# Building the one-hot factors of the expert gates: the gate moved from B to A, and the work shared out anew among VectorE, ScalarE and GpSimd

## The chip, the cores and the metric

The kernel runs on one core of one Trainium2 chip. The time is the device time of one execution in microseconds (us); the number given for a kernel is the median of several executions.

## What is computed

The reference is one transformer block over 1024 tokens of width 1024 (16 meta tokens are put in front and dropped at the end): half of the mixing channels go through a chunked mLSTM, half through attention with a forget gate, and then comes a product-key expert layer (PEER) with 16,384 one-neuron experts. The change touches only the expert layer:

```python
def _peer(x, w_query, sub_keys, u_emb, v_emb):
    ...
        scores = jnp.einsum('thpc,hpnc->thpn', qh, keys32)
        val, idx = lax.top_k(scores, PEER_TOPK)
        ...
        top_s, pos = lax.top_k(cand, PEER_TOPK)
        ids = jnp.take_along_axis(cand_id, pos, axis=-1).reshape(tb, PEER_HEADS * PEER_TOPK)
        gate = jax.nn.softmax(top_s, axis=-1).reshape(tb, PEER_HEADS * PEER_TOPK)
        u = u_emb[ids]
        act = jax.nn.gelu(jnp.einsum('ted,td->te', u, xb).astype(jnp.float32), approximate=False)
        w = (gate * act).astype(xb.dtype)
        return jnp.einsum('te,ted->td', w, v_emb[ids])
```

Each token picks 8 heads x 16 = 128 experts. An expert's number is 128*i + j, with i and j from 0 to 127, and each pick has a gate, which is never negative because it comes out of a softmax.

## The kernel before

The 1024 tokens are four segments of 256 (two blocks of 128 each). Segments 0 and 3 take the expert layer by **gathering**: for each of a token block's 128 picks one indirect DMA, issued on GpSimd's queue (POOL), brings 128 rows of `peer_u` (tile `gu`, L329, 512 KB), and VectorE (DVE) multiplies and sums it (L338); later 128 rows of `peer_v` per token (tile `gv`, L365) are summed by TensorE (PE) into `po` (L387), four tokens per batch. The gathers of segment 0 run beside the earlier stages and are still under way in the stage looked at here; those of segment 3 are spread over the last stage by a pacer (`Paced`, L1025), each asked for after a given PE instruction.

Segments 1 and 2 (`DENSE`) take it **densely**: all 16,384 experts are computed for their 512 tokens, and the results are weighed with a matrix of gates that is zero but for the 128 picks. `gates()` (L1118) expands the picks into this matrix. It takes the i, the j and the gate of a block of 128 tokens, transposed so that a pick is a partition and a token a column (`iT`, `jT`, `gT`), and goes through the tokens in groups of four. Per token there are two 128 x 128 factors with one row per pick: A holds a 1 in column i, B the gate in column j. One matmul (L1163, tile `gout`, in fp32 two instructions in the trace) sums the product over the picks and leaves the token's 128 x 128 gates in PSUM. ScalarE (ACT) copies the four results into `G` (L1165), and every 32 tokens `G` goes to DRAM (`gd`, 2 MB). A, B and the PSUM tile `gout` have two buffers each.

Who makes what for a group of four tokens, before: DVE makes A of three tokens in one comparison of 128 x 384 (L1153); ACT makes A of the fourth in two instructions, |column - i| (L1156) and relu(1 - that) (L1157); B is made per token by one instruction that compares and multiplies by the gate (L1161), on POOL for the first token (`GPOOL = 1`) and on DVE for the other three.

What stands around it: `merge` (L1194) interleaves the expert search of segment 3 (`topk`: projections on PE, maxima on DVE), some dense projections kept for later (`spill`) and the 16 steps of `all_gates`. A scheduler then sets each engine's order for good; every engine runs its instructions in that order, so an instruction that waits holds up all behind it on its engine. After the gates comes the **last stage** (from L1216): per four rows of experts, `Gt` is read back from `gd` (L1232), multiplied into the expert activations (L1236), split into two halves `Wh` and `Wl` (L1239, L1240), and PE multiplies with `peer_v` (`vo`, L1258) between projections of `peer_u` (`du`, L293); DVE adds `vo` to the result (L1263).

Gather tiles come from two pools of 7 and 4 buffers (`GATH`, `GATHV`). For the second token block of segment 0 even batches of `gv` take the one pool and odd ones the other (`room0`, L1005).

Of the kernel before, what the change touches and what calls it, by code (L numbers as in the profile page):

```python
# [9 lines left out]
F32 = mybir.dt.float32  # L10
# [3 lines left out]
AF = mybir.ActivationFunctionType  # L14
OP = mybir.AluOpType
# [4 lines left out]
P = 128  # L20
# [25 lines left out]
DENSE = (1, 2)  # L46
# [9 lines left out]
TOP0 = (0, 1, 0, 1)  # L56
SW = 1
GP0 = 5
GACT = 1
GPOOL = 1  # L60
T3W = 1.2
GW = 1
T00 = 0
# [30 lines left out]
def _block_kernel(ctx, tc, nc, I, out, dbg):  # L94

    def pool(name, bufs, stack=ctx, **kw):
        return stack.enter_context(tc.tile_pool(name=name, bufs=bufs, **kw))
# [27 lines left out]
    def bank(name):  # L125
        turn_b[0] += 1
        if extra is not None and turn_b[0] % XB == 0:
            return extra[:, turn_b[0] // XB % 2, :]
        return ps.tile([P, 512], F32, tag="bank", name=name, bufs=2)
# [9 lines left out]
    dve, act, pe, pool_e, sync = nc.vector, nc.scalar, nc.tensor, nc.gpsimd, nc.sync  # L139
# [34 lines left out]
    iota = cp.tile([P, P], F32, tag="iota", name="iota")  # L174
# [897 lines left out]
    for i in range(-1, len(SEGS)):  # L1072
# [9 lines left out]
        if i >= 0:  # L1082
            S = segs[i]
# [34 lines left out]
    def gates(S, gb):  # L1118

        for b in range(NB):  # L1120
            hi = gb.tile([P, P], I32, tag="gi", name="gi_hi")
            lo = gb.tile([P, P], I32, tag="gi", name="gi_lo")
            dve.tensor_scalar(hi, S.idx[:, b, :], 7, None, op0=OP.logical_shift_right)
            dve.tensor_scalar(lo, S.idx[:, b, :], 127, None, op0=OP.bitwise_and)
            T = []
            for x, nm in ((hi, "iT"), (lo, "jT"), (None, "gT")):
                if x is None:
                    f = S.gate[:, b, :]
                else:
                    f = gb.tile([P, P], F32, tag="gf", name="gf", bufs=1)  # L1130
                    dve.tensor_copy(f, x)
                tb = bank("gtr")
                with tc.high_priority():
                    pe.transpose(tb[:, 0:P], f, ident)
                t_ = gb.tile([P, P], F32, tag=nm, name=nm, bufs=1)
                act.copy(t_, tb[:, 0:P])
                T.append(t_)
            iT, jT, gT = T
            if GACT:
                niT = gb.tile([P, P], F32, tag="niT", name="niT", bufs=1)  # L1140
                act.mul(niT, iT, -1.0)
            for tg in range(P // TG):
                G = gb.tile([P, P, TG], F32, tag="G", name="G")
                for q in range(TG // 4):
                    bk = dps.tile([P, 512], F32, tag="db", name="gout")
                    t0 = tg * TG + q * 4
                    ts4 = slice(t0, t0 + 4)
                    A = gb.tile([P, 4, P], F32, tag="A", name="A")
                    B = gb.tile([P, 4, P], F32, tag="B", name="B")
                    bc = [P, 4, P]  # L1150
                    io = iota.unsqueeze(1).broadcast_to(bc)
                    nd = 4 - GACT
                    dve.tensor_tensor(A[:, 0:nd], io[:, 0:nd], iT[:, t0:t0 + nd].unsqueeze(2).broadcast_to([P, nd, P]),  # L1153
                                      op=OP.is_equal)
                    for u in range(nd, 4):
                        act.activation(A[:, u, :], iota, AF.Abs, bias=niT[:, t0 + u:t0 + u + 1])  # L1156
                        act.activation(A[:, u, :], A[:, u, :], AF.Relu, bias=1.0, scale=-1.0)  # L1157
                    for u in range(4):
                        t1 = slice(t0 + u, t0 + u + 1)
                        e = pool_e if u < GPOOL else dve  # L1160
                        e.tensor_scalar(B[:, u, :], iota, jT[:, t1], gT[:, t1], op0=OP.is_equal, op1=OP.mult)  # L1161
                        with tc.high_priority():
                            pe.matmul(bk[:, u * P:(u + 1) * P], B[:, u, :], A[:, u, :], start=True, stop=True)  # L1163
                    with nullcontext():
                      act.copy(G[:, :, q * 4:q * 4 + 4].rearrange("p i t -> p t i"),  # L1165
                             bk.rearrange("p (t i) -> p t i", t=4))
                sync.dma_start(gd[(NB * (S.sg - DENSE[0]) + b) * (P // TG) + tg], G)
                yield
# [20 lines left out]
    gb = pool("gbuild", 2, gbs, reuse_waits="tile")  # L1189
    def all_gates():  # L1190
        for d in DENSE:
            yield from gates(segs[d], gb)
# [130 lines left out]
```

## Time and profile before

| | us |
|---|---|
| median of 3 runs | 3425.85 (3422.84 to 3432.39) |
| the execution that was profiled | 3424.24 |
| its span, which all times of the trace are measured in | 3422.4 |
| PE busy with matmuls | 3040.1 (89%) |
| DVE busy | 2294.6 (67%) |
| POOL busy | 1523.4 (45%) |
| ACT busy | 1066.8 (31%) |

Times of the trace count from the start of the span, which is 1.84 us shorter than the execution. A share over the whole span says little here: stages with different limits follow one another. The gates run from 1642 to 2111 us. Until 1907 PE has the projections of the search and the spill to do beside them, and from 1907 to 2111 it has only gates and gathered rows. The last stage's first `vo` matmul starts at 2128.4 and the stage lasts to the end.

A row of instructions in the profile reads: line, engine, operation, output<-inputs, shape, count | busy time, mean ns of one | idle time of the engine just before them, and what ended it. SPq is the queue of SyncE, from which most DMAs are issued.

### The profile page before, as it was taken

How to read it: one execution, taken by the hardware profiler on the slowest of the kernel's cores; microseconds unless marked ns; L12 is line 12 of the kernel's file. 1: busy time of each engine (PE TensorE's matmuls, PEld its weight loads, DVE VectorE, ACT ScalarE, POOL GpSimd, SP SyncE). 2: the span in 40 equal slices, each digit the busy share in tenths (PEclk: the TensorE clock that was granted, in tenths of full speed). 3: DMA queues.
4: the chain of work that ended last, by engine and by line, in shares of the span. 5: the costliest groups of instructions: out<-in, count | busy, mean ns of one | idle time of the engine just before them, and what ended most of it. 6: DMA issues, size and time to landing. Idle time of an engine off the chain costs nothing. (4 is left out here: it accounts for less than half of the span.)

```text
span 3422.4 us, 42278 instructions
## 1 busy us (share of the span) xinstructions
PE 3040.1 (89%) x14225; PEld 2220.2 (65%) x14225; DVE 2294.6 (67%) x5970; ACT 1066.8 (31%) x2007; POOL 1523.4 (45%) x1321
## 2 busy tenths in 40 slices
PE   8899899878768868999998775999999999999999
PEld 4566677545535646676766553777777777777666
DVE  3242678577667999776788546788767677775443
ACT  1323424233333212222444553222322232322221
POOL 1000011177875777433565675454444545444442
PEclk9998899879679888999998886999999999999999
DMA  4444445579989999866787887888889999998995
GB/s 135 131 126 137 144 145 149 167 240 315 250 299 331 328 334 346 252 242 234 283 325 280 316 302 284 287 311 314 307 310 344 345 348 343 353 342 308 339 333 205
DMA packets 373821, 931.23 MB, mean 272 GB/s; under 512 B 57268, under 2 KB 143508, under 8 KB 371556
## 3 DMA queue, kind: packets, MB, share of 16 engines
q0 software_dynamic: 161216, 552.56, 45.9%
q1 hardware_dynamic: 212388, 375.96, 32.7%
q8 instruction: 113, 1.85, 0.2%
q14 instruction: 104, 0.85, 0.1%
HBM read 860.91 MB, written 67.47 MB: 271 GB/s over the span
## 5 line engine op out<-in xcount | busy, mean ns | idle before, releaser
L329 POOL DMA_INDIRECT gu<-in_peer_u,idx x512 | 626.3, 1223 | 521.1 <-PE vo L1258 110.0
L365 POOL DMA_INDIRECT gv<-in_peer_v,idT x512 | 546.0, 1066 | 593.1 <-PE po L387 314.3
L338 DVE SCALAR_TENSOR_TENSOR gu<-gu,xng 128x1024 f32<-128x1024 f32 x472 | 592.5, 1274 | 62.5 <-DMA gu<-in_peer_u,idx 60.6
L282 ACT CAST wh<-raw 128x1024 fp32r<-128x1024 f32 x288 | 302.1, 1049 | 884.2 <-PE vo L1258 270.9
L287 DVE TENSOR_TENSOR wl<-raw,wh 128x1024 fp32r<-128x1024 f32 x262 | 320.5, 1223 | 283.0 <-ACT wh L282 250.5
L1258 PE MATMUL vo<-wh,Wh 128*128 128x512 f32 x1024 | 376.7, 396 | 34.9 <-ACT Wh L1239 18.1
L1258 PE MATMUL vo<-wl,Wh 128*128 128x512 f32 x1024 | 402.6, 393 | 0.0
L1258 PE MATMUL vo<-wh,Wl 128*128 128x512 f32 x1024 | 400.3, 392 | 0.0
L387 PE MATMUL po<-gv,Z 128*32 128x512 f32 x2048 | 262.7, 606 | 19.1 <-DMA gv<-in_peer_v,idT 18.9
L306 PE MATMUL fp<-hnh,raw 128*128 128x256 f32 (+1 forms) x1024 | 251.4, 404 | 22.3 <-DVE frs L633 11.3
L1258 PEld LDWEIGHTS vo<-wh,Wh 128*128 128x128 f32 x1024 | 194.1, 190 | 98.3 <-issue 23.3
L293 PE MATMUL du<-xl,wh 128*128 128x512 f32 x640 | 250.3, 391 | 0.0
L293 PE MATMUL du<-xh,wl 128*128 128x512 f32 x640 | 250.2, 391 | 0.0
L293 PE MATMUL du<-xh,wh 128*128 128x512 f32 x640 | 249.8, 390 | 0.0
L306 PEld LDWEIGHTS fp<-hnh,raw 128*128 128x128 f32 x1024 | 203.8, 203 | 60.5 <-DVE frs L633 12.7
L1258 PEld LDWEIGHTS vo<-wl,Wh 128*128 128x128 f32 x1024 | 193.8, 189 | 48.6 <-issue 8.4
L1258 PEld LDWEIGHTS vo<-wh,Wl 128*128 128x128 f32 x1024 | 193.2, 189 | 48.1 <-issue 7.5
L1163 PE MATMUL gout<-A,B 128*128 128x128 f32 x1024 | 164.0, 319 | 67.6 <-POOL B L1161 62.9
L1163 PEld LDWEIGHTS gout<-A,B 128*128 128x128 f32 x1024 | 150.9, 226 | 103.6 <-POOL B L1161 76.6
L1165 ACT COPY G<-gout 128x512 f32<-128x512 f32 x128 | 136.4, 1066 | 202.0 <-PE gout L1163 195.4
L433 PE MATMUL tk<-raw,hnh 128*128 128x512 f32 (+1 forms) x416 | 197.4, 623 | 2.0 <-ACT vp L576 1.8
L1263 DVE TENSOR_TENSOR acc<-acc,vo 128x512 f32<-128x512 f32 x256 | 167.0, 683 | 32.8 <-PE vo L1258 29.1
(409 smaller groups left out, 5397.5 us busy)
## 6 DMA issues: line engine op xcount, KB each, us to landing
raw<-in_ut SPq DMA_DIRECT2D x128, 512.0 KB
raw<-in_peer_v SPq DMA_DIRECT2D x128, 512.0 KB
raw<-in_wf SPq DMA_DIRECT2D x64, 512.0 KB
gd<-G SPq DMA_DIRECT2D x16, 2048.0 KB
Gt<-gd SPq DMA_DIRECT2D x32, 1024.0 KB
raw<-in_wt SPq DMA_DIRECT2D x48, 512.0 KB
raw<-in_wq SPq DMA_DIRECT2D x48, 512.0 KB
raw<-in_wo SPq DMA_DIRECT2D x32, 512.0 KB
```

The costliest lines, as they stand in the source:

```text
L282: seen["act"] = act.copy(h, raw)
L287: seen["dve"] = dve.tensor_sub(l, raw, h.bitcast(F32))
L293: seen["pe"] = pe.matmul(o, w, x[:, c], start=(first and i == 0), stop=(last and i == 2))
L306: pe.matmul(o, raw[:, k * P:(k + 1) * P], xh[:, k, c], start=(k == 0), stop=(k == KT - 1))
L329: d = pool_e.indirect_dma_start(out=t, out_offset=None, in_=I["peer_u"], in_offset=bass.IndirectOffsetOnAxis(ap=S.idx[:, lb, r:r + 1], axi ...
L338: dve.scalar_tensor_tensor(t, t, 1.0, xn[0], op0=OP.mult, op1=OP.mult, accum_out=G.actv[:, r:r + 1])
L365: d = pool_e.indirect_dma_start(out=t, out_offset=None, in_=I["peer_v"], in_offset=bass.IndirectOffsetOnAxis(ap=S.idT[lb][:, tok:tok + 1], ...
L387: last = pe.matmul(G.po[32 * q_:32 * q_ + 32, n, :], z[:, q_, 31 - j:63 - j], rows[q_][:, n * 512:(n + 1) * 512], start=(j == 0), stop=(j ...
L433: pe.matmul(b[0:w, :], xh[:, k, s0:s0 + w], raw[:, k % 2 * 512:(k % 2 + 1) * 512], start=(k == 0), stop=(k == KT - 1))
L1163: pe.matmul(bk[:, u * P:(u + 1) * P], B[:, u, :], A[:, u, :], start=True, stop=True)
L1258: seen["pe"] = pe.matmul(bks[b], w[:, cw], v, start=(ii == 0 and i == 0), stop=(ii == GRP - 1 and i == 2))
L1263: dve.tensor_add(o, o, bks[b])
```

## The change

The gate is multiplied into A, not into B. B is then a bare comparison and is made for all four tokens in one DVE instruction of 128 x 512. A is made per token: the fourth by ACT, whose second instruction now is relu(g - g*|column - i|) with the gate and the negated gate (`ngT`, new) as operands read per partition; the others by an instruction that compares and multiplies, as B was before, on POOL for the first token of a group in the first dense segment, and on DVE for the rest. In the second dense segment POOL makes nothing.

```diff
-GACT = 1
-GPOOL = 1
+
+GPOOL = (1, 0)
...
-            if GACT:
-                niT = gb.tile([P, P], F32, tag="niT", name="niT", bufs=1)
-                act.mul(niT, iT, -1.0)
+            niT = gb.tile([P, P], F32, tag="niT", name="niT", bufs=1)
+            act.mul(niT, iT, -1.0)
+            ngT = gb.tile([P, P], F32, tag="ngT", name="ngT", bufs=1)
+            act.mul(ngT, gT, -1.0)
...
-                    nd = 4 - GACT
-                    dve.tensor_tensor(A[:, 0:nd], io[:, 0:nd], iT[:, t0:t0 + nd].unsqueeze(2).broadcast_to([P, nd, P]),
-                                      op=OP.is_equal)
-                    for u in range(nd, 4):
-                        act.activation(A[:, u, :], iota, AF.Abs, bias=niT[:, t0 + u:t0 + u + 1])
-                        act.activation(A[:, u, :], A[:, u, :], AF.Relu, bias=1.0, scale=-1.0)
+                    dve.tensor_tensor(B, io, jT[:, t0:t0 + 4].unsqueeze(2).broadcast_to(bc), op=OP.is_equal)
                     for u in range(4):
                         t1 = slice(t0 + u, t0 + u + 1)
-                        e = pool_e if u < GPOOL else dve
-                        e.tensor_scalar(B[:, u, :], iota, jT[:, t1], gT[:, t1], op0=OP.is_equal, op1=OP.mult)
+                        if u == 3:
+
+                            act.activation(A[:, u, :], iota, AF.Abs, bias=niT[:, t1])
+                            act.activation(A[:, u, :], A[:, u, :], AF.Relu, bias=gT[:, t1], scale=ngT[:, t1])
+                        else:
+                            e = pool_e if u < GPOOL[S.sg - DENSE[0]] else dve
+                            e.tensor_scalar(A[:, u, :], iota, iT[:, t1], gT[:, t1], op0=OP.is_equal, op1=OP.mult)
```

Since the scheduler orders all engines anew, three places are shown. In the changed kernel the lines behind the diff are one higher. On **POOL**, at the end of the gates, there stood before (x is the number of instructions in a row; `gv` and `gu` are the gathers):

```order
L1161 TENSOR_SCALAR B<-iota,jT,gT 128x128 x6
L365 DMA gv<-in_peer_v,idT 128x1024 x5
L1161 TENSOR_SCALAR B<-iota,jT,gT 128x128
L329 DMA gu<-in_peer_u,idx 128x1024 x2
L1161 TENSOR_SCALAR B<-iota,jT,gT 128x128 x7
L365 DMA gv<-in_peer_v,idT 128x1024 x4
L1161 TENSOR_SCALAR B<-iota,jT,gT 128x128
L329 DMA gu<-in_peer_u,idx 128x1024 x3
L1161 TENSOR_SCALAR B<-iota,jT,gT 128x128
L329 DMA gu<-in_peer_u,idx 128x1024 x3
L1161 TENSOR_SCALAR B<-iota,jT,gT 128x128 x4
L329 DMA gu<-in_peer_u,idx 128x1024 x6
```

and now, from the last steps of the first dense segment on:

```order
L365 DMA gv<-in_peer_v,idT 128x1024 x7
L1162 TENSOR_SCALAR A<-iota,iT,gT 128x128
L365 DMA gv<-in_peer_v,idT 128x1024
L1162 TENSOR_SCALAR A<-iota,iT,gT 128x128 x6
L365 DMA gv<-in_peer_v,idT 128x1024 x61
L329 DMA gu<-in_peer_u,idx 128x1024 x2
L365 DMA gv<-in_peer_v,idT 128x1024 x4
L329 DMA gu<-in_peer_u,idx 128x1024 x126
```

Every factor that stood between the gathers of the second dense segment is gone, and only two `gu` stand ahead of the last four `gv`, where there were two ahead of them and seventeen more among the factors behind.

On **PE**, at the change from the gates to the last stage (`gout` here counts one instruction a token, `po` eight a batch of four tokens; `idt` are two small transposes), before:

```order
L1163 MATMUL gout<-A,B 128x128 x5
L387 MATMUL po<-gv,Z_139 32x512 x6
L1163 MATMUL gout<-A,B 128x128 x3
L387 MATMUL po<-gv,Z_139 32x512 x2
L1163 MATMUL gout<-A,B 128x128 x16
L387 MATMUL po<-gv,Z_141 32x512 x8
L1163 MATMUL gout<-A,B 128x128 x8
L360 MATMUL idt<-identr,idf 128x128
L1163 MATMUL gout<-A,B 128x128 x8
L360 MATMUL idt<-identr,idf 128x128
L1163 MATMUL gout<-A,B 128x128 x20
L1258 MATMUL vo<-wh,Wh 128x512
```

and now:

```order
L387 MATMUL po<-gv,Z_139 32x512 x8
L1164 MATMUL gout<-A,B 128x128 x26
L387 MATMUL po<-gv,Z_141 32x512 x8
L1164 MATMUL gout<-A,B 128x128 x4
L387 MATMUL po<-gv,Z_139 32x512 x8
L1164 MATMUL gout<-A,B 128x128 x38
L387 MATMUL po<-gv,Z_141 32x512 x8
L387 MATMUL po<-gv,Z_139 32x512 x8
L387 MATMUL po<-gv,Z_141 32x512 x8
L387 MATMUL po<-gv,Z_139 32x512 x8
L1259 MATMUL vo<-wh,Wh 128x512
```

The gates now end before the gathered rows: four batches of `po` stand between the last gate and the first `vo`, where before the gates were last. From the last `du` of the search part on there are 17 batches and 67 groups of four tokens before, 16 batches and 64 groups now.

On **DVE**, at the same change of stage (`gu` is the gathered product of segment 3, `Z` a small copy for a batch of `po`), before:

```order
L1153 TENSOR_TENSOR A<-iota,iT 128x384
L1161 TENSOR_SCALAR B<-iota,jT,gT 128x128 x3
L338 SCALAR_TENSOR_TENSOR gu,actv<-gu,xng 128x1024 x5
L1236 TENSOR_TENSOR w<-w,Gt 128x512 x4
L1240 TENSOR_TENSOR Wl<-w,Wh 128x512 x3
L1236 TENSOR_TENSOR w<-w,Gt 128x512 x2
L1240 TENSOR_TENSOR Wl<-w,Wh 128x512 x3
L1236 TENSOR_TENSOR w<-w,Gt 128x512 x3
L1240 TENSOR_TENSOR Wl<-w,Wh 128x512 x2
L287 TENSOR_TENSOR wl<-raw,wh 128x1024
L338 SCALAR_TENSOR_TENSOR gu,actv<-gu,xng 128x1024 x3
L1263 TENSOR_TENSOR acc<-acc,vo 128x512 x4
```

and now:

```order
L1153 TENSOR_TENSOR B<-iota,jT 128x512
L1162 TENSOR_SCALAR A<-iota,iT,gT 128x128 x3
L381 COPY Z_141<-wT 128x4
L381 COPY Z_139<-wT 128x4
L338 SCALAR_TENSOR_TENSOR gu,actv<-gu,xng 128x1024
L381 COPY Z_141<-wT 128x4
L338 SCALAR_TENSOR_TENSOR gu,actv<-gu,xng 128x1024
L1237 TENSOR_TENSOR w<-w,Gt 128x512 x4
L1241 TENSOR_TENSOR Wl<-w,Wh 128x512 x3
L1237 TENSOR_TENSOR w<-w,Gt 128x512 x2
L1241 TENSOR_TENSOR Wl<-w,Wh 128x512 x3
L287 TENSOR_TENSOR wl<-raw,wh 128x1024
```

The `gu` products of segment 3 moved behind the change of stage: counted from the start, 236 of the 472 on DVE stood ahead of the end of the first four `acc` additions, and now 223. The lag of 13 is made up by the 52nd addition (338 in both), some six groups of experts later.

## The prediction

> **What bounds the kernel now.** I start with the 40 slices of the page, 85.6 us each, and then cut the span at the changes of stage.
>
> ```profile
> PE   8899899878768868999998775999999999999999
> PEclk9998899879679888999998886999999999999999
> ```
>
> ```profile
> 1642.00:1907.00 265.00, 243.79 (x1426) 181.90 (x1424) 228.09 (x932) 117.65 (x236) 153.69 (x147) 0.95 0.80 297
> 1907.00:2111.00 204.00, 135.24 (x816) 95.87 (x814) 112.10 (x310) 106.22 (x214) 149.64 (x141) 0.80 0.80 296
> 2111.00:2128.40 17.40, 0.02 (x1) 0.02 (x1) 4.31 (x9) 1.07 (x3) 0.00 (x0) 0.59 0.98 342
> 2128.40:2440.00 311.60, 294.77 (x1266) 241.47 (x1267) 262.92 (x393) 87.34 (x111) 144.35 (x112) 0.98 0.87 304
> 2440.00:3422.40 982.40, 975.89 (x4730) 716.71 (x4728) 593.43 (x871) 271.33 (x349) 418.30 (x381) 1.00 0.89 324
> ```
>
> The columns are length, busy time of PE, its weight loads, DVE, ACT and POOL, then granted clock, DMA share and GB/s. PE is full in the last stage: from 2440 on it has work for 976 of 982 us. So the end of the kernel moves with the start of that stage, 2128.4. Ahead of it PE is busy for only 135 of 204 us, and no other engine is full. I call 1907 to 2128.4, 221.4 us, the **tail**. PE's and DVE's waits in it, then POOL's work:
>
> ```profile
> PE gout L1163 <- POOL B L1161: 57.6, 28, 8.7
> DVE A L1153 <- PE gout L1163: 75.4, 42, 6.6
> L1161 POOL TENSOR_SCALAR B<-iota,jT,gT 128x128 f32<-128x128 f32 x65 | 69.2, 1067 | 21.0 <-PE gout L1163 19.2 <-DMA gv<-in_peer_v,idT 0.5 <-POOL B L1161 0.2
> L365 POOL DMA_INDIRECT gv<-in_peer_v,idT x57 | 57.4, 1008 | 26.5 <-PE po L387 14.2 <-issue 9.7 <-PE gout L1163 2.3
> L329 POOL DMA_INDIRECT gu<-in_peer_u,idx x19 | 23.0, 1213 | 4.7 <-issue 3.4 <-DVE B L1161 0.5 <-DVE A L1153 0.5
> ```
>
> PE waits 57.6 us for a factor from POOL, and DVE waits for PE because the buffers of A and B are not free. The factor's own 1.07 us isn't the trouble; its place is, behind gathers that wait for buffers. One round on POOL:
>
> ```profile
> 1975.20 1.02 POOL L365 DMA_INDIRECT gv<-in_peer_v,idT  x1 [1.86 <-PE po L387]
> ...
> 1979.08 0.95 POOL L365 DMA_INDIRECT gv<-in_peer_v,idT  x1 [0.30 <-PE po L387]
> 1980.07 1.57 POOL L1161 TENSOR_SCALAR B<-iota,jT,gT 128x128 f32<-128x128 f32 x2
> ...
> 1995.46 1.02 POOL L365 DMA_INDIRECT gv<-in_peer_v,idT  x1 [1.86 <-PE po L387]
> ```
>
> Gathers wait for `po` on PE, `po` stands behind `gout`, `gout` waits for factors behind gathers: 20.3 us for eight gathers (1975.20 to 1995.46).
>
> **Part 1, the tail: gates without POOL.** The 64 groups of four tokens left in the tail need nothing of POOL any more. What then bounds a group is read where no gather was in the way:
>
> ```profile
> 1948.03 0.56 DVE L1153 TENSOR_TENSOR A<-iota,iT 128x384 f32<-128x384 f32 x1 [0.21 <-PE gout L1163]
> 1948.51 0.92 DVE L1161 TENSOR_SCALAR B<-iota,jT,gT 128x128 f32<-128x128 f32 x3
> 1949.50 0.56 DVE L1153 TENSOR_TENSOR A<-iota,iT 128x384 f32<-128x384 f32 x1
> ```
>
> DVE needs 0.48 us from the comparison's start to the next instruction and 0.99 for the three others: 1.47 a group. The comparison grows from 384 to 512 columns. The trace has none of 128 x 512; its nearest rows are one of 400 and a product of 512:
>
> ```profile
> L947 DVE TENSOR_TENSOR oh<-iota,posf 128x400 f32<-128x400 f32 x32 | 18.5, 578 | 0.3
> L1236 DVE TENSOR_TENSOR w<-w,Gt 128x512 f32<-128x512 f32 x128 | 86.1, 685 | 21.7 <-DMA Gt<-gd 14.1 <-ACT w L1185 6.0 <-ACT w L1182 1.4
> ```
>
> It adds between 0.02 (578 less 557) and 0.13 us (685 less 557); I take 0.13, since the 512 columns agree: 1.60 a group on DVE. On ACT only the second instruction changes, to operands per partition:
>
> ```profile
> L1156 ACT ACTIVATE A<-iota,niT 128x128 f32<-128x128 f32 x128 | 50.2, 393 | 0.0
> L1157 ACT ACTIVATE A<-A 128x128 f32<-128x128 f32 x128 | 37.1, 310 | 1.7
> ```
>
> It costs 310 ns now and 393 at most, what the one with such a bias costs (its nearest row; no less than 310 either, since only operands are added). ACT's round, 1.46 us between these two, becomes 1.54 and stays below DVE's:
>
> ```profile
> 1948.04 0.39 ACT L1156 ACTIVATE A<-iota,niT 128x128 f32<-128x128 f32 x1
> 1949.50 0.40 ACT L1156 ACTIVATE A<-iota,niT 128x128 f32<-128x128 f32 x1
> ```
>
> Engines alone would do 64 groups in 102 us. **DMA forbids that.** What the tail moved:
>
> ```profile
> DMA packets 18187, 66.54 MB, mean 300 GB/s; under 512 B 1615, under 2 KB 5453, under 8 KB 17021
> ```
>
> By POOL's order two `gu` are left ahead of the last `gv` instead of 19, so 17 x 0.524 = 8.9 MB go to the last stage and 57.6 MB stay: gathers, `G`, `Gt`. At what rate? Three stretches with the DMA engines full:
>
> ```profile
> 1740.00:1760.00 20.00, 19.84 (x122) 14.66 (x115) 18.94 (x78) 7.81 (x15) 16.27 (x16) 1.00 1.00 376
> 1920.00:1940.00 20.00, 11.72 (x73) 7.53 (x74) 7.56 (x22) 11.09 (x20) 14.39 (x16) 0.76 1.02 409
> 2671.00:2711.00 40.00, 40.00 (x192) 30.30 (x191) 28.73 (x44) 13.36 (x18) 21.88 (x20) 1.00 1.04 391
> ```
>
> That is 384 GB/s at a share of 1.00. The tail now runs at 0.80. Without POOL in the loop I take 0.93, between that and full, since the stage's last 17 us run at 0.98: 357 GB/s, and 57.6 MB take 161 us. The tail shrinks by **60 us**. The bounds: 192 us (-29) if the mean stays at 300 GB/s, 139 us (-82) at 415 GB/s, a little over the best of the three. A check by rounds: 16 batches of four gathers at 20.3 us for two are 162 us.
>
> The hand-over is not shortened. The last `G` is written and `Gt` read back before the first `vo`:
>
> ```profile
> 2111.43 0.32 SPq L1167 DMA_DIRECT2D gd<-G  x1
> 2128.38 0.79 PE L1258 MATMUL vo<-wh,Wh 128*128 128x512 f32 x1 [18.09 <-ACT Wh L1239]
> ```
>
> These 17 us now lie beside the four batches of `po` that PE's order puts between the last gate and the first `vo`; they cost something only if the gathers end first.
>
> What hides a gather's issue? Nothing on POOL stands in front of it now, but DVE gets denser. The 57 `gv` took 1008 ns each here, with DVE busy for 55% of the time, and between 1642 and 1907, with DVE busy for 86%:
>
> ```profile
> L365 POOL DMA_INDIRECT gv<-in_peer_v,idT x81 | 82.5, 1019 | 59.2 <-PE po L387 28.6 <-issue 12.7 <-PE gtr L1134 9.1
> ```
>
> 11 ns more, so I charge nothing; a stretch to twice the time is a rival below. [...]
>
> **Part 2, 1642 to 1907.** POOL still makes one factor a group there; DVE makes two per token instead of three (374 ns mean here, 63 groups: -23.6 us) and the longer comparison (+8.2 us). DVE has 15 us less to do, but PE is busy for 244 of 265 us. Bounds 0 and -8 on the better side, and +5 if ACT's 0.083 x 63 counted; I take **-2 us**. The new `ngT` is four small ACT copies, under 2 us in all, hidden in that.
>
> **Part 3, the start of the last stage.** The order on DVE moves 13 `gu` products behind the change of stage. PE waits there for DVE already:
>
> ```profile
> PE vo L1258 <- DVE acc L1263: 16.8, 7, 4.1
> L338 DVE SCALAR_TENSOR_TENSOR gu<-gu,xng 128x1024 f32<-128x1024 f32 x114 | 135.3, 1219 | 2.5 <-DMA gu<-in_peer_u,idx 2.5
> ```
>
> 13 x 1.22 = 16 us more for an engine that is busy for 263 of 312 us. If the slack took them all the cost is 0, if none it is 16. I take **+10 us**, nearer the upper end since PE waits for just this engine. After 2440 nothing waits for DVE, and the sum ends there.
>
> **Sum**, against the profiled execution: 3422.4 of span and 1.8 around it are 3424.2; -60 - 2 + 10 = -52 gives 3372.2. The median of the runs lies 1.6 above that execution: **3374 us**.
>
> **The rivals.**
>
> *DMA does not speed up* (17%). The tail keeps its 300 GB/s because eight gathers in flight, waiting for buffers, set the rate and not POOL: -29 - 2 + 10, 3405. For it: PE still takes `po` in order. Against it: POOL's own wait for `po` is 14.2 us of 204.
>
> *Engines alone set the pace* (13%): -82, with little of part 3 felt, 3347. For it: 409 GB/s over 20 us. Against it: `G` and the gathers would have to keep that up for 139.
>
> *Gathers stretched by DVE* (5%). This row has DVE's products beside the issue:
>
> ```profile
> 2079.45 2.11 POOL L329 DMA_INDIRECT gu<-in_peer_u,idx  x1 [0.16 <-DVE B L1161]
> ```
>
> At 2.11 + 0.30 us an issue a round of eight takes 19.3 us and some 2 to 5 for landing and `po`; seven and a half rounds (half a round is under way at the start) at 23 us end 12 us later than forecast: 3386. [...]
>
> *POOL was not what held the gates* (6%): the change does not do what it says, PE's 57.6 us turn up as waits for DVE or ACT, and the pace stays at 204/67 = 3.0 us a group: 3418 to 3436. Against it: the 1.47 us groups at 1948, with DVE and ACT as now.
>
> *Slower: one batch at a time* (9%). The place is PE's order, where `po` for a batch stands ahead of 26 to 53 gates. If only one batch of four is in flight, each costs its issue, its landing and its sum. A landing in the trace:
>
> ```profile
> 1666.80 1.09 POOL L365 DMA_INDIRECT gv<-in_peer_v,idT  x1 [0.31 <-issue]
> 1675.19 1.92 PE L387 MATMUL po<-gv,Z 128*32 128x512 f32 x16 [1.57 <-DMA gv<-in_peer_v,idT]
> ```
>
> 4 x 1.31 + 7.3 + 1.9 = 14.4 us a batch, 16 batches 231 us, 10 more than the tail has now; with all 16 us of part 3 the time is 3450. It decides from 13 us a batch on. Against it: even and odd batches take different pools, and now two batches take 20.3 us together.
>
> **How the numbers follow.** The forecast has 50%, with 3358 to 3390 of its own. Faster by over 0.3% (10 us, about what a measurement of this kernel tells from no change): 50 + 17 + 13 + 5 less 1, 84%; within: 7%; slower: 9%. The range 3340 to 3410 leaves out the slower case, no change and the ends of the two rivals beside the forecast.
>
> **What would show it.** In the profile after: no POOL among PE's waits after the search (else POOL was not removed); a group of gates at 1.6 us where no `po` stands between; a DMA share of 0.9 or more there; the first `vo` near 2066; `vo` waiting for `acc` for 20 to 33 us before 2440. The forecast is wrong if PE's `po` waits for `gv` long enough to hold up the gates, or if the last stage starts early and then waits for `gu`.

## The result, and the profile after

The changed kernel takes **3339.9 us** (median of 4 runs, 3335.47 to 3347.03) against 3428.85 for the kernel before (4 runs, 3422.84 to 3432.39) beside it: a ratio of 0.9744, with a 95% interval of 0.9721 to 0.9768. The profiled execution took 3335.47 us, with a span of 3333.7. The prediction had the sign and its main term, but 3374 is too high: the measured time lies below the forecast's own 3358 to 3390 and right at the lower end of the stated range, 3340 to 3410.

The two rows of the page's 40 slices, now 83.3 us each:

```profile
PE   8999899868767867899999976999999999999999
PEclk9998899978778888899999998999999999999999
```

The weak stretch of before (8775 in slices 22 to 25) is down to two slices (76 in 24 and 25). By stages, in the view by windows (length, busy time of PE, its weight loads, DVE, ACT and POOL, granted clock, DMA share, GB/s), cut at the end of the last `du` of the search, at the last gate, at the first `vo`, and 300 us on:

```profile
1642.00:1890.00 248.00, 240.04 (x1469) 180.44 (x1467) 225.37 (x886) 137.18 (x255) 164.81 (x148) 0.99 0.85 315
1890.00:2013.60 123.60, 96.86 (x694) 69.86 (x697) 90.69 (x257) 105.53 (x198) 48.72 (x48) 0.96 0.93 362
2013.60:2042.60 29.00, 8.97 (x64) 2.25 (x63) 4.28 (x10) 1.84 (x3) 10.85 (x12) 0.71 1.03 388
2042.60:2342.00 299.40, 289.12 (x1245) 233.03 (x1246) 269.71 (x412) 85.13 (x109) 165.15 (x126) 0.98 0.94 343
2342.00:3333.70 991.70, 985.01 (x4768) 723.68 (x4767) 604.76 (x886) 273.41 (x351) 423.99 (x385) 1.00 0.90 324
```

The search stage ended 17.3 us earlier (1907.3 before), the tail fell from 221.1 to 152.6 (-68.5), and the last stage from 1294.0 to 1291.1 (-2.9): together -88.7, all of the gain. In the tail PE's waits, and below them the costliest group of POOL, read:

```profile
PE po L387 <- DMA gv<-in_peer_v,idT: 19.3, 3, 16.1
PE gout L1164 <- ACT G L1166: 14.8, 23, 3.0
PE gout L1164 <- ACT A L1159: 5.2, 9, 0.8
PE gout L1164 <- DVE A L1162: 3.2, 8, 0.4
```

```profile
L365 POOL DMA_INDIRECT gv<-in_peer_v,idT x57 | 57.3, 1006 | 94.4 <-PE po L387 80.4 <-issue 8.2 <-PE gout L1164 5.2
```

The 57.6 us that PE waited for a factor of POOL are gone, and POOL does nothing but issue gathers and wait for their buffers (80.4 us). What is late now is many things by a little, and one wait of 16.1 us. That one is at the hand-over, in PE's timeline:

```profile
2013.50 3.64 PE L387 MATMUL po<-gv,Z 128*32 128x512 f32 x32
2033.23 5.43 PE L387 MATMUL po<-gv,Z 128*32 128x512 f32 x32 [16.09 <-DMA gv<-in_peer_v,idT]
2042.63 0.50 PE L1259 MATMUL vo<-wh,Wh 128*128 128x512 f32 x1 [3.96 <-ACT Wh L1240]
```

After the last gate two batches of `po` run at once. Their buffers then come free, five `gv` and two `gu` gathers are issued on POOL (2015.67 to 2023.13), and PE stands still until the `gv` for the next two batches have landed.

### The profile page after: what moved, and what is told of

The parts are those of the page before. It is cut to its first block, busy times and chain, and to the rows that moved or that the text cites. A ratio compares the mean times of both kernels' runs of the same rounds, so it can differ in the third digit from the quotient of the medians.

```text
span 3333.7 us, 42081 instructions
## 1 busy us (share of the span) xinstructions
PE 3010.5 (90%) x14225; PEld 2194.4 (66%) x14225; DVE 2287.0 (69%) x5906; ACT 1086.3 (33%) x2011; POOL 1465.8 (44%) x1257
## 4 chain that ended last, share of the span: by engine, by line
PE 67%; DVE 15%; DMA 9%; ACT 4%; issue 3%; POOL 3%; SPq 0%; ACTq 0%; POOLq 0%; DVEq 0%
PE vo L1259 21%; PE du L293 12%; PE tk L433 7%; PE po L387 7%; PE fp L293 5%; DVE gu L338 4%; PE fp L306 4%; DMA gv<-in_peer_v,idT 3%; PE gout L1164 2%; PE q L293 2%; DMA gu<-in_peer_u,idx 1%; PE pv L787 1%; PE q L306 1%; DMA raw<-in_wq 1%; POOL gu L329 1%
## 5 line engine op out<-in xcount | busy, mean ns | idle before, releaser
L306 PEld LDWEIGHTS fp<-hnh,raw 128*128 128x128 f32 x1024 | 203.5, 202 | 60.6 <-DVE frs L633 12.7
L1240 ACT CAST Wh<-w 128x512 fp32r<-128x512 f32 x128 | 79.2, 621 | 277.9 <-PE vo L1259 150.5
L733 POOL DMA_DIRECT2D kqa<-kd x32 | 22.7, 709 | 330.2 <-ACT pt L779 220.5
L1164 PEld LDWEIGHTS gout<-A,B 128*128 128x128 f32 x1024 | 130.7, 196 | 56.3 <-ACT G L1166 24.1
```

Source lines behind the costliest of these rows:

```text
L306: pe.matmul(o, raw[:, k * P:(k + 1) * P], xh[:, k, c], start=(k == 0), stop=(k == KT - 1))
```

## Experiments

All lengths below are read as in this table, from the profile of each run: the search stage from the first `gi_hi` (L1123) to the end of the last `du`, the tail from there to the first `vo`, the last stage from there to the end of the span.

| kernel | search | tail | last stage | median us |
|---|---|---|---|---|
| before | 275.0 | 221.1 | 1294.0 | 3428.85 |
| before, profiled again | 267.7 | 218.6 | 1300.5 | 3420.03 (1 run) |
| changed | 257.5 | 152.6 | 1291.1 | 3339.90 |
| POOL in both segments | 260.2 | 220.3 | 1296.5 | 3415.81 |
| old division, POOL in the first | 268.6 | 172.9 | 1281.5 | 3358.78 |
| Relu with constant scale | 272.9 | 157.3 | 1292.1 | 3355.93 |
| no ACT in the second | 256.9 | 169.7 | 1285.4 | 3346.02 |
| Relu constant, same order | 256.1 | 149.2 | 1292.1 | 3333.28 |
| before's order, less DVE | 263.2 | 220.5 | 1297.2 | 3422.19 |
| ACT light, same order | 258.6 | 151.7 | 1290.4 | 3333.48 |
| no POOL at all | 273.2 | 156.3 | 1280.2 | 3349.75 |
| half of the gate writes, same order | 262.5 | 150.7 | 1310.1 | 3362.91 |
| less DVE, same order | 260.5 | 155.1 | 1293.3 | 3347.85 |
| `gu` products cut, same order | 258.9 | 152.9 | 1298.4 | 3351.93 |

### Was it GpSimd in the tail, or the new division of the work?

```diff
-GPOOL = (1, 0)
+GPOOL = (1, 1)
```

> The changed kernel, with GpSimd making its one A of four in the second dense segment too (the new division of the work kept, GpSimd not taken out of the loop of the gathers). Theory (GpSimd's A beside its gathers is what held the gates of the tail): the tail from the last search product to the first `vo` goes back from 152.6 us to about 220, the search stage stays at about 248, in all about 3405 us; `gout` waits for `A` of POOL in the tail by 50 us or more. Rival (the new division of the work between VectorE and ScalarE is what shortened the tail): the tail stays within 10 us of 153, in all about 3340.

The tail is 220.3 us, and the ratio to before 0.9961 (0.9946 to 0.9977); the time, 3415.81, lies 11 us above the expected 3405, and in the profile 10 us of that stand ahead of the gates, which begin at 1642.7 instead of 1632.5. PE's longest waits in the tail:

```profile
PE gout L1164 <- POOL A L1162: 57.5, 26, 9.2
PE vo L1259 <- ACT Wh L1240: 28.3, 1, 28.3
```

The old wait is back almost to the tenth of a microsecond (57.6 before). The other half of the change alone, on the kernel before:

```diff
-                        e = pool_e if u < GPOOL else dve
+                        e = pool_e if u < GPOOL and S.sg == DENSE[0] else dve
```

> The kernel before, with GpSimd making its B of four in the first dense segment alone; VectorE makes all four B in the second, and the gate stays in B. Theory (GpSimd beside the gathers held the gates of the tail): the tail falls from 221 us to 150 to 165 (VectorE then has four tensor_scalars and the comparison of three A, more than ScalarE's 1.65 us a group, so it may stay some us above the changed kernel's 152.6), the search stage stays at 265, in all about 3360. Rival (division of the work): the tail stays near 220, in all about 3425.

The ratio is 0.9795 (0.9775 to 0.9814): of some 88 us of gain this one line brings about 70, with the old factors, and POOL is gone from PE's waits in the tail. The tail, 172.9 us, stays 8 us above the range expected. Its gates take 132.0 us (203.8 before, 123.6 in the changed kernel), but the hand-over takes 40.9, of which PE waits 14.7 for gathers and 13.2 for `Wh`. Both runs say that GpSimd's factors among the gathers held the gates. The division of the work has the rest, or the order that came with it.

What the runs don't separate is the place of the factors and the time that they take. In the tail before, 65 of them kept POOL busy for 69.2 us, about as much as the tail lost. In the round of eight gathers that the prediction shows (1975.20 to 1995.46) POOL waited for PE for 3.6 of 20.3 us and was taken up by gathers and factors for the rest. Factors cut short, in the same order, would tell the two apart; that was not run.

### Does the pace of VectorE and ScalarE set the tail now?

```diff
-                        if u == 3:
+                        if u == 3 and S.sg == DENSE[0]:
```

> The changed kernel, with all four A of a group made by VectorE in the second dense segment, none by ScalarE there. VectorE's group: one comparison of 690 ns and four tensor_scalars, about 1.9 us, against ScalarE's 1.65 now. Theory A (the pace of the gates sets the tail): some 60 groups of the tail at +0.2 to +0.25 us, 12 to 15 us more in the tail, in all about 3352. Theory B (the transfers set it): the tail within 3 us of 152.6, in all about 3340.

The tail is 169.7 us, 17 more, in the direction of theory A, but not by its mechanism. The gates end at 2012.9 and take 126.2 us, against 123.6; the hand-over has grown, from 29 to 44. PE's timeline there:

```profile
2026.74 4.91 PE L387 MATMUL po<-gv,Z 128*32 128x512 f32 x32 [13.85 <-DMA gv<-in_peer_v,idT]
2041.47 3.64 PE L387 MATMUL po<-gv,Z 128*32 128x512 f32 x16 [9.81 <-DMA gv<-in_peer_v,idT]
```

PE's order here has one more batch of `po`, and so one more round of gathers, ahead of the first `vo`; the changed kernel has its last batch behind it, at 2060.87. The last stage, which has that batch no more, is 5.7 us shorter.

In the changed kernel ScalarE's second instruction was longer than predicted. Its groups in the gates, with VectorE's comparison (mean ns behind the comma):

```profile
L1159 ACT ACTIVATE A<-A,gT,ngT 128x128 f32<-128x128 f32 x61 | 29.2, 493 | 1.2
L1158 ACT ACTIVATE A<-iota,niT 128x128 f32<-128x128 f32 x60 | 23.3, 392 | 2.5 <-PE gout L1164 2.5
L1153 DVE TENSOR_TENSOR B<-iota,jT 128x512 f32<-128x512 f32 x61 | 42.1, 690 | 18.5 <-PE gout L1164 16.8 <-ACT jT L1136 1.4
```

Since a gate is at most 1, relu(gate - |column - i|) is the same factor with a constant scale:

```diff
-act.activation(A[:, u, :], A[:, u, :], AF.Relu, bias=gT[:, t1], scale=ngT[:, t1])
+act.activation(A[:, u, :], A[:, u, :], AF.Relu, bias=gT[:, t1], scale=-1.0)
```

> The changed kernel, with the second activation of ScalarE as Relu(gate - |difference|), its scale the constant -1, in place of Relu(gate - gate times |difference|) with a scale for each partition; the gates are at most 1, so the A is the same. Theory A (ScalarE's 1.65 us a group sets the pace of the gates, and these the tail): Relu falls from 492 ns to about 390, the group to 1.55 us, the tail by 4 to 8 us, in all 3328 to 3336 us. Theory B (the transfers set the tail): Relu falls as well, but the tail stays within 2 us of 152.6 and the time within 2 us of the changed kernel's 3339.9. A third outcome: Relu stays near 492, so that the pointer of the bias is its price, not that of the scale, and nothing changes.

Relu fell to 402 ns, and the kernel became slower than the changed one: 3355.93, a miss for all three outcomes. The search stage is 15 us longer. The scheduler sets the order by its own estimate of durations, and after this edit, which also drops the four small copies to `ngT`, the order is another one: 64 groups of gates stand ahead of the last `du` instead of 66, and yet PE waited 15 us in the stage (8 in the changed kernel) and was busy 7 us longer for 17 matmuls fewer. So the same change of the scale was made once the order was set, on the instructions themselves:

```diff
+for i in instructions_in_their_final_order:
+    if i is Relu and reads ngT as its scale:
+        scale of i = -1.0
```

> The same edit as in the run before (Relu with the constant scale -1), but made after the scheduler has set the order, so that every engine has the changed kernel's order, instruction for instruction. That run had Relu at 402 ns instead of 494 and was 16 us slower than the changed kernel, 19 of them before the last search product. Theory (the order that the scheduler found was to blame, not the cheaper instruction): the search stage ends within 3 us of 1890.0, and the tail is 3 to 8 us shorter than 152.6, since ScalarE's group falls by 0.09 us: 3332 to 3340 us. Rival (the cheaper instruction itself shifts the waits of the search stage): its last product is late by 10 us or more again, 3350 or more.

The search stage is 256.1 us and the tail 149.2. The time is 3333.28, a ratio to before of 0.9734 (0.9710 to 0.9758); against 0.9787 (0.9770 to 0.9803) in the other order. So the order cost the 16 us, and not the cheaper instruction. Against the changed kernel the intervals overlap: if it is better, it is by too little to tell. To see what a much lighter ScalarE gives, its two instructions were cut to 8 columns in the second segment, again in the final order:

```diff
+for i in instructions_in_their_final_order, second dense segment:
+    if i is Abs or Relu of the fourth A:
+        columns of i = 8
+    if i is the fourth product:
+        A of i = the third A
```

> The changed kernel in its own order, but with ScalarE's two instructions for the fourth A cut from 128 columns to 8 in the second dense segment (the product of the fourth token reads the third one's A, so part of the gates is left out): ScalarE's group falls from 1.65 us to about 1.45 or less, and VectorE's 1.38 is as long. Theory (the pace of the gates sets the tail): 64 groups at 0.2 us, the tail 10 to 15 us shorter, 3325 to 3330 us. Rival (the transfers are the floor, at a share of 0.95): at most 4 us, 3336 or more.

The tail is 151.7 us, 0.9 less. The groups, and what PE waited for the copy of `G` in the gates:

```profile
L1159 ACT ACTIVATE A<-A,gT,ngT 128x8 f32<-128x8 f32 x61 | 23.0, 391 | 1.2
L1158 ACT ACTIVATE A<-iota,niT 128x8 f32<-128x8 f32 x62 | 17.9, 292 | 3.1 <-PE gout L1164 3.1
```

```profile
PE gout L1164 <- ACT G L1166: 13.6, 28, 2.7
```

Where no `po` stands between, a group did fall from 1.65 to 1.45 us, so ScalarE sets the pace there:

```profile
1907.49 0.29 ACT L1158 ACTIVATE A<-iota,niT 128x8 f32<-128x8 f32 x1
1908.94 0.28 ACT L1158 ACTIVATE A<-iota,niT 128x8 f32<-128x8 f32 x1
```

The gates as a whole took 121.8 us, against 123.6. Pairs of batches of `po` came as far apart as in the changed kernel (16.7 to 25.6 us; 16.8 to 26.1 there). ScalarE waited 24 us for a product to copy instead of 14, PE waited almost as long for the copy of `G` as before (14.8), `po` waited in the gates for gathers for 4.6 us instead of 3.2, and PE was busy for 99.2 us instead of 96.9, at a granted clock of 0.93 instead of 0.96. So the theory of the gates' pace misses. The time, 3333.48, lies between the two expectations (3325 to 3330, and 3336 or more). The theory of the transfers has its own test next.

### Do the transfers set it?

```diff
+for i in instructions_in_their_final_order:
+    if i writes gates to DRAM, second dense segment:
+        columns of i = 2048
+    if i reads gates from DRAM:
+        blocks of i = the first one, 16 times
```

> The changed kernel in its own order, but the eight last writes of the gates to DRAM (the second dense segment's) carry half of their columns, 1 MB each instead of 2, and the reads of the gates take the first block's each time; so part of the gates is left out. That takes some 8 MB from the 56.0 MB that the tail moves. Theory (the tail lasts as long as its transfers: 56 MB at 367 GB/s): 20 to 23 us shorter, about 131 us, in all 3314 to 3320 us. Rival (the engines, or PE's order of `po` and gates, set it): at most 5 us, 3333 or more. Between them: the transfers until the engines' 64 groups at 1.65 us and a hand-over of some 20 us take over, 125 to 140 us.

What the tail moved, first in the changed kernel, then here:

```profile
DMA packets 15147, 55.98 MB, mean 367 GB/s; under 512 B 1332, under 2 KB 4679, under 8 KB 14067
```

```profile
DMA packets 14917, 47.84 MB, mean 317 GB/s; under 512 B 1343, under 2 KB 4371, under 8 KB 13830
```

The tail by windows, first in the changed kernel, then here (the last two numbers are the DMA share and GB/s):

```profile
1890.00:2042.60 152.60, 105.83 (x754) 72.11 (x753) 94.97 (x267) 107.36 (x200) 59.56 (x60) 0.91 0.95 367
1899.50:2050.20 150.70, 106.27 (x754) 71.42 (x753) 94.81 (x267) 107.47 (x200) 62.03 (x62) 0.92 0.84 316
```

8.1 MB went, the DMA engines' share fell from 0.95 to 0.84, and the tail is 150.7 us instead of 152.6. So the transfers alone are not the floor. A run that lightens them and ScalarE together was not made. The time as a whole, 3362.91, is 23 us above the changed kernel's, which neither side expected: the last stage grew by 19 us, with PE waiting 12.0 us in it for VectorE's `acc`. The gates that it reads are all from one block in this run; whether that is why was not tried. The stage ahead of the gates was late by 4.5 us too (last section).

### The search stage: less work for VectorE, or another order?

The kernel before in its own order, VectorE's comparison cut to one token's 128 columns in the first dense segment, and the kernel before unchanged:

```diff
+for i in instructions_in_their_final_order, first dense segment:
+    if i is the comparison for A:
+        columns of i = 128
+    if i is the second or third product:
+        A of i = the first A
```

> The kernel before in its own order, instruction for instruction, but with VectorE's comparison in the first dense segment made for one token instead of three (the products of the second and third token read the first one's A, so part of the gates is left out): some 0.27 us less for each of 64 groups, about 17 us less for VectorE in the search stage, where the changed kernel had 15 us less by the count of its instructions. Theory (less work for VectorE is what shortened the search stage by 17 us): its last product comes 10 to 17 us before 1907, in all 3412 to 3418 us. Rival (it was the order of the work, not its amount): 0 to 4 us, in all 3424 to 3428.

> The kernel before, profiled once more, to see how far its search stage varies by itself: the run with less work on VectorE in this order had its last search product at 1894 us in its profile, 13 us earlier than the first profile of the kernel before (1907), while its median was only 5 us lower. If VectorE's work makes the difference: 1905 to 1909 again. If the stage varies by itself by as much: anywhere from 1893 to 1905.

The last starts of `du` in the search, with less work and in the second profile of the kernel before:

```profile
L293 PE MATMUL du<-xh,wl x8: 389/390/395, 1887.4 to 1893.9; 128*128 128x512 f32 x8
```

```profile
L293 PE MATMUL du<-xh,wl x8: 388/389/395, 1892.3 to 1898.8; 128*128 128x512 f32 x8
```

The unchanged kernel itself ended this stage 8 us earlier than in its first profile. So of the 17 us between the first pair of profiles up to 8 are the spread of the kernel before, and 17 us less work gave 4.5 to 12 us in single profiles, and a ratio of 0.9989 (0.9973 to 1.0005): 4 us by the ratio, with an interval from a gain of 9 us to a loss of 2. Neither expectation holds in both its stage and its time. In the changed kernel's order, with a larger cut:

```diff
+for i in instructions_in_their_final_order, first dense segment:
+    if i is the comparison for B:
+        columns of i = 128
+    if i is the second, third or fourth product:
+        B of i = the first B
```

> The changed kernel in its own order, but VectorE's comparison made for one token instead of four in the first dense segment (all four products read that B, so part of the gates is left out): about 0.4 us less for each of 64 groups, 26 us less for VectorE in the search stage. Theory (VectorE's work still decides that stage): its last product comes 8 us or more before 1890.0, in all 3332 or less. Rival (the stage is set by PE, busy for 240 of 248 us in this order): 0 to 4 us, in all 3335 to 3340.

The search stage is 260.5 us, not shorter than 257.5, so VectorE does not decide it in this order. The median, 3347.85, lies above both expectations; the profile is 12.7 us longer than the changed kernel's, with 5 of these ahead of the gates, 3 in the search stage, 2.5 in the tail and 2 in the last stage. Last, all of GpSimd's factors to VectorE:

```diff
-GPOOL = (1, 0)
+GPOOL = (0, 0)
```

> The changed kernel with GpSimd making no A in the first dense segment either; VectorE makes three there. VectorE gets 64 instructions of about 0.37 us more in the search stage (24 us), where it is busy for 225 of 248 us. Theory (VectorE's share of the work decides the search stage): it grows by 10 to 20 us, in all 3350 to 3360. Rival (GpSimd's factors behind gathers hold up the search stage too, or the order decides): no change or a gain, 3325 to 3342.

The search stage is 273.2 us, 16 longer. That agrees with the theory, but since the scheduler made a new order here as well, and an order alone was worth 15 us above, it is no proof: PE has 1603 matmuls in this stage instead of 1505, and is busy for 260.7 us instead of 249.3, which is 11 of the 16 us. What helps in the tail, GpSimd without factors, at least brings nothing in the first segment.

### The products moved into the last stage

```diff
+for i in instructions_in_their_final_order:
+    if i is one of the gu products 224 to 239 on VectorE:
+        columns of i = 64
```

> The changed kernel in its own order, with 16 of VectorE's `gu` products right behind the change of stage (the 224th to the 239th) cut from 1024 columns to 64, so part of the expert activations is left out. About 1.1 us less for each, 17 us less for VectorE in the first 50 us of the last stage: as much work as the 13 products that the change moved there. Theory (those products fit into time in which VectorE only waited, so they cost the last stage nothing): from the first `vo` to the end within 4 us of the changed kernel's 1291.1, which two more profiles in that order gave as 1290.4 and 1292.1. Rival (they do cost some 10 us as predicted, and something else in the new order gives more back): the last stage is 8 to 12 us shorter, 1279 to 1283.

The last stage is 1298.4 us, not shorter. PE's longest wait in it:

```profile
PE vo L1259 <- ACT wh L282: 10.5, 2, 9.4
```

Taking 16 us of products from VectorE saved nothing; the stage is even 7 us longer, with a wait for ScalarE of 10.5 us that is 3.1 in the changed kernel. Behind it ScalarE itself waited for a read of `peer_v`, 8.1 us against 0.7 there. VectorE's wait for ScalarE is the other thing that changed:

```profile
ACT wh L282 <- DMA raw<-in_peer_v: 8.1, 1, 8.1
DVE wl L287 <- ACT wh L282: 29.5, 17, 8.4
```

That is 29.5 us in the first 300 of the stage against 9.7 in the changed kernel, 8.4 of them in one wait behind the late read: with less of the products VectorE stands idle for longer. The rival (they cost 10 us) finds nothing for it, and without the late read the stage would be, by estimate, as long as the changed kernel's (1298.4 less 7.4 is 1291.0). Why the read was late was not tried, so the cost of nothing is likely, and not shown within the 4 us asked for.

## Why the prediction was right, and where it was wrong

Against the profiles the sum was -52 and the measured change -88.7. Of the 37 us between them 8.5 are in part 1, 15 in part 2 and 13 in part 3, all on the same side. The first `vo` came at 2042.6, not near 2066.

**Part 1, the tail: the sign and the size held, the floor did not.** Forecast -60 us, measured -68.5 (-66 against the second profile of before). That GpSimd's factors among the gathers held the gates is shown by the two runs that put them back and that took them away alone. That it was their place and not their own time, as the prediction has it, is argued and not shown. What the text asked for is there: no POOL among PE's waits in the tail, a share of 0.93 in the gates, and a group at 1.65 us where no `po` stands between, read off ScalarE's timeline:

```profile
1906.67 0.40 ACT L1158 ACTIVATE A<-iota,niT 128x128 f32<-128x128 f32 x1
1907.11 0.49 ACT L1159 ACTIVATE A<-A,gT,ngT 128x128 f32<-128x128 f32 x1
1907.51 1.01 ACT L1166 COPY G<-gout 128x512 f32<-128x512 f32 x1
1908.32 0.39 ACT L1158 ACTIVATE A<-iota,niT 128x128 f32<-128x128 f32 x1
```

That this meets the 1.6 asked for is luck: the 1.60 was VectorE's round, which took 1.37 us here (its comparisons start at 1907.08 and 1908.45), and the 1.65 is ScalarE's.

The step of 57.6 MB at 357 GB/s also met its numbers (55.98 at 367). That is luck too, for the claim over it, "DMA forbids that", is not borne out: 8.1 MB less shortened the tail by 1.9 us only. Nor does ScalarE set it alone: with its group 0.2 us shorter the tail is 0.9 us shorter. So the rival of the engines alone, 3347 and nearest in number, is not borne out either; a lighter VectorE was not tried in the tail. What is left is read from the trace and not shown by a run: PE is busy for 96.9 of the gates' 123.6 us, alternates `po` with groups of gates in a set order, and waits some 40 times for up to 3.0 us, mostly for ScalarE; then come 29 us of hand-over, a round of gathers long. A limit that no run touched is the gathers' own round: a batch's buffers come free with its `po` (POOL waited 80.4 us of the tail for `po`), and the next `po` of that pool can't run before they are filled again (PE waited 19.3 us for `gv`). The forecast hid the hand-over beside the gathers; it is the part that the order made longer (17 before, 29 here, 44 without ScalarE's share). Whether a third buffer of `gout`, or `po` ahead of the last gates, would take those waits away was not tried.

**ScalarE's Relu lay outside its bounds.** "393 at most" took the row of an instruction with one operand per partition; with two it is 492. A third row, 310 with none, was there to show the step: +83 for the first, and as much again for the second gives 476, an estimate. Measured were 310 ns with none, 392 to 402 with one and 492 with two. The longer Relu made ScalarE's group the longest instead of VectorE's, and cost nothing that could be told from the spread of the runs. The comparison of 128 x 512 was 690 ns, as forecast (0.69).

**Part 2, the search stage, was mis-sized:** -2 forecast, with -8 to +5 as bounds; -17 measured against the first profile, -10 by the table against the second. (Where the prediction says that VectorE makes two factors per token instead of three, it means per group of four tokens; its -23.6 us is reckoned so.) VectorE's smaller share is worth about 4 us by the runs in the old order, so inside those bounds. The rest most likely came by a way that the sum had no term for: the scheduler's order. Nearly the same instructions in another order were 15 to 17 us apart in this stage. How the gain divides between the two can't be settled within the spread of the profiles.

**Part 3 had the wrong sign:** +10 forecast, -2.9 measured (-9 against the second profile). The step that failed is "nearer the upper end since PE waits for just this engine". The 16.8 us that PE waited for `acc` were real, but VectorE was not full. Its own waits for ScalarE in the first 300 us of the last stage, first before, then after:

```profile
DVE wl L287 <- ACT wh L282: 31.9, 27, 2.9
DVE Wl L1240 <- ACT Wh L1239: 12.5, 13, 2.7
```

```profile
DVE wl L287 <- ACT wh L282: 9.7, 14, 1.7
DVE Wl L1241 <- ACT Wh L1240: 6.7, 6, 2.9
```

VectorE waited 44 us for ScalarE there, and 16 now. So it was most likely its order and not its work that made `acc` late, and the moved products filled idle time; the run that cut such products, where VectorE idled again and `vo` waited for `acc` for 0.5 us only, agrees. `vo` now waits for `acc` for 0.2 us, where 20 to 33 us were forecast. The 263 of 312 us that the prediction quoted said as much: 49 were free. The gain is only 2.9 us because other waits came in its place: in the whole stage PE waited 16.8 us for `acc` before, and 10.5 us for one thing or another after (5.7 of them in one wait for `Wl`), and one batch of `po` more, 3.6 us, lies in the stage.

**The rivals.** Transfers went at 367 GB/s and not 300; a `gv` took 1006 ns in the tail (1008 before), and 1015 in its gates, where VectorE was busy for 73% of the time, so the gathers were not stretched; batches still went in pairs.

## What to carry to other kernels

An instruction that stands among gathers on one queue can hold up every engine that needs its result, even where its own engine looks far from full: 65 factors of 1.07 us, on an engine busy for 73% of the time, cost some 70 us here. When one engine waits for another, look at what the second one waits for before charging it with more work. And where a scheduler orders by estimated durations, compare a small edit in one and the same order, since another order alone moved this kernel by 16 us, more than most edits are worth.

## What the runs showed of the hardware

The code ahead of the change has the same order in several of these kernels, and still took from 322.2 to 331.6 us to the first addition to `h2b` on VectorE. In the changed kernel and in the run with the cut `gu` products, both in the same order, 120 to 200 us reads:

```profile
120.00:200.00 80.00, 70.74 (x279) 47.80 (x278) 36.71 (x117) 31.75 (x93) 5.48 (x8) 0.94 0.51 138
```

```profile
120.00:200.00 80.00, 70.24 (x254) 48.30 (x253) 35.44 (x114) 29.78 (x84) 5.49 (x8) 0.87 0.51 134
```

The granted clock (third from the end) is 0.94 in one and 0.87 in the other, and PE got 279 matmuls done in the one and 254 in the other: 0.07 of 80 us are 5.6 us, an estimate of what this stretch has of the 9.4 us between these two. One and the same order met different clocks; what sets the clock is not shown. Stages, not ends, have to be compared for this reason.
